# A hybrid trunk layer on one core: six small moves ahead of the MLP, a VectorE-only MLP passage, and another order of the second MLP product

## The chip, the cores and the metric

The kernel runs on one core of a Trainium2 chip. The metric is the device time of one execution in microseconds (us), the median of several runs. PE is TensorE's matmul side, PEld its weight loads, DVE is VectorE, ACT is ScalarE, POOL is GpSimd, SP issues nearly all the DMAs.

## The reference

One layer for 1024 prompt tokens and 8 x 16 sample tokens, 1152 in all, model width 1024, fp32:

```python
x = layer_norm(x, ln_in_g, ln_in_b)
proj = x @ w_in                      # 1024 -> 5920, split among four head groups
# A: Mamba-2 SSD with a causal conv of width 4     B: mLSTM, 4 heads
# C: RG-LRU, 512 channels, causal conv             D: gated linear attention (GLA), 4 heads
x = layer_norm(alpha * x + concat(A, B, C, D) @ w_out, ln1_g, ln1_b)
hid = square(relu(x @ w1 + b1))      # 1024 -> 4096
x = layer_norm(alpha * x + hid @ w2 + b2, ln2_g, ln2_b)
```

The outputs are x for prompt and sample tokens and eight recurrent states for each.

## The kernel before, in words

Every fp32 product is computed in three passes: an operand is split into a rounded part (`hi`, a copy on ACT) and the rest (`lo`, a subtraction on DVE), and `mm3` multiplies hi by hi, hi by lo and lo by hi into one PSUM bank. A split of a 128 x 1024 weight tile is thus one ACT copy and one DVE subtraction.

The stages follow each other: `dense_first` (input LayerNorm, transposes, the first three blocks of w_in, one of 384 token columns at a time), the rest of the input projection with the four mixers' steps woven in by `tick()` (every 12 matmuls a tick runs as many pending steps as the ticks left call for), the out-projection `dense_tm` in five groups of w_out rows, the first MLP product, and the second.

Both MLP products use a scheme of seven products of half-size blocks in place of eight, with sums and differences of blocks as operands. For the first, `x_first` and `x_rest` split the token side (tiles `xo`: A11, A12, then S1 to S4 and A22; the sums stand in `s` and in place in `x`) and `q_prep` the weights (tiles `wq`, split into `wo`: B11, B21, T1, T2, T3, T4, B22). `mlp_a(j)` runs the two products that need only A11 and A12, `mlp_b(j)` the other five. The stretch between the out-projection and the end of `x_rest(3)`, in which `mlp_a(0)` to `mlp_a(3)` run while the sums are made, is called the passage here. Its sums and splits are shared by DVE and POOL: the difference in place of `x`, the `lo` parts of S3 and A22 and all `wq` differences are POOL's.

The second product takes its operands from DRAM (`hid_d`, the sums `s_d`, the weight sums `t_d`) in units (p, u): product p, 256 rows u of the contraction. `load_to` and `prep_to` fetch four and split three units ahead. All eight product slots run over u = 0 to 5 first (`CHUNKS[0]`), then over u = 6, 7 as the tail; product slot 0 feeds the sample tokens only. The evacuated parts collect in `a1`, `a5`, `a6`, and in the rows `top`, `bot`, `smp`, which start as the residual (`res_make`, on POOL). The tail ends tile by tile with product 5, then 7, then 4, and the second LayerNorm (`ln_stats2`, `ln_a`, `ln_b`, `ln_g`, `ln_c`, `ln_stt`) is spread over DVE, ACT and POOL.

The order on each engine is made by a list scheduler from the program order and its priorities (`tc.high_priority()`); in the last stretch and in the first (`pinned`) program order is kept. Each engine then runs its list strictly in order. Large tiles come from one pool of 38 slots (`S`), the PSUM banks from a pool of 3 (`pd`) and one of 5 (`pm`).

All engine calls are made through one helper, so every row shows its line, L66 in the kernel before and L62 in the changed one.

Of the kernel before, what the change touches and what calls it, by code (L numbers as in the profile page):

```python
# [13 lines left out]
P = 128  # L14
NTOK = 1152
NT = 9
# [23 lines left out]
STT = (7, 6)  # L40
NG5 = 0
PIN = 'VATG'
LOG = ((4, 0), (4, 1))
CHUNKS = (tuple(range(6)), (6, 7))
# [6 lines left out]
def tile_trunk(ctx: ExitStack, tc: tile.TileContext, I, O, dbg=None):  # L51
# [665 lines left out]
    def conv_block(store, key, st_in, nrow, ch0, wcol, bcol, act, o_p, o_s, early=False):  # L717
# [11 lines left out]
        def evac(c, ps):  # L729
            if c == 0:  # L730
                raw = S("raw", (P, SW))
                d["raw"] = raw
                V.memset(raw[:, 0:3], 0.0)
                sv = raw[:, 1027:1179].rearrange("p (b s) -> p b s", s=19)
                d["sv"] = sv
                cs = d["cs"] if early else load()
                pt = pm("pcs")
                T.transpose(pt[:, 0:24], cs[0:24, :], ident[0:24, 0:24])
                A.activation(sv[:, :, 0:3], pt[:, 0:24].rearrange("p (b j) -> p b j", j=3), AF.Copy)
            raw = d["raw"]  # L740
# [36 lines left out]
        def state():  # L777
            raw, sv = d["raw"], d["sv"]
            cs = Dt("cso", 27)
            A.activation(cs[:, 0:3], raw[:, PT:PT + 3], AF.Copy)  # L780
            A.activation(cs[:, 3:27].rearrange("p (b j) -> p b j", j=3), sv[:, :, LS:LS + 3], AF.Copy)
            pt = pm("pco")
# [298 lines left out]
    def ml_steps(h):  # L1081
# [22 lines left out]
        def stB(i):  # L1104
# [41 lines left out]
            y = Dt("y", P)  # L1146
            A.activation(y, ti[:, 0:P], AF.Square, scale=r[:, 0:1], accum_out=r[:, 1:2])
# [3 lines left out]
            G.tensor_scalar(y, ti[:, 0:P], r[:, 3:4], None, op0=OP.mult)  # L1151
            d["y", i] = y
# [36 lines left out]
        for s in range(NT + 3):  # L1189
            def f(s=s):  # L1190
# [6 lines left out]
                if 3 <= s <= NT + 2:  # L1197
                    stC(s - 3)
# [97 lines left out]
    def gl_steps(p):  # L1296
# [21 lines left out]
        def stB(i):  # L1318
# [3 lines left out]
            if i < 8:  # L1322
# [11 lines left out]
                if i:  # L1334
                    G.tensor_scalar(St, St, sc[:, 1, i:i + 1], None, op0=OP.mult)
                    V.scalar_tensor_tensor(St, pS, sc[:, 2, i:i + 1], St, op0=OP.mult, op1=OP.add)
                else:
                    V.tensor_scalar(St, pS, sc[:, 2, 0:1], None, op0=OP.mult)
                if i < 7:
                    for h in range(2):  # L1340
                        hs = slice(64 * h, 64 * h + 64)
                        V.tensor_scalar(glB[hs, h, :], St[hs], sc[hs, 0, i + 1:i + 2], None, op0=OP.mult)
# [129 lines left out]
    def rg_steps(j):  # L1472
# [15 lines left out]
        def gates(c):  # L1488
            def f():
# [7 lines left out]
                if c < 2:  # L1497
                    split(c + 1)
# [45 lines left out]
        return [g0] + [w] * 5 + [gates(0)] + [w] * 0 + [gates(1)] + [w] * 0 + [gates(2), e1, e2, e3]  # L1544
# [86 lines left out]
    def w2_sums():  # L1631
# [3 lines left out]
        for k in range(KF // 2):  # L1635
            for c in (0, 256):
# [17 lines left out]
                def f3(sub=sub, store=store):  # L1654
# [3 lines left out]
                    sub("21", "22", "21")  # L1658
# [133 lines left out]
    def x_split(name, k, src, e=V):  # L1792
# [3 lines left out]
        e.tensor_tensor(t[:, 1, :], src, t[:, 0, :], op=OP.subtract)  # L1796
# [5 lines left out]
    def x_rest(k):  # L1802
# [31 lines left out]
    def q_prep(j):  # L1834
# [7 lines left out]
        def sub(dst, a, b):  # L1842
            G.tensor_tensor(wq[dst, j], wq[a, j], wq[b, j], op=OP.subtract)
# [126 lines left out]
    for g, n in enumerate(GR):  # L1970
# [4 lines left out]
        for i in range(NT):  # L1975
# [65 lines left out]
    mlp_a(0, firsts(1))  # L2041
    q_first(2)
    rest_cm(0, 1)
    x_rest(0)
    mlp_a(1, firsts(2))
    q_first(3)
    rest_cm(2)
    x_rest(1)
    q_load(0)
    mlp_a(2, firsts(3))  # L2050
    rest_cm(3)
    prep[0].pop(0)()
    x_rest(2)
    prep[0].pop(0)()
    q_load(1)
    mlp_a(3, lambda: None)
    prep[0].pop(0)()
# [37 lines left out]
    order, order_end = (1, 5, 6, 4, 0, 7, 2, 3), (2, 3, 0, 1, 6, 5, 7, 4)  # L2095
    tail = CHUNKS[-1]
    units = [(p, u) for us in CHUNKS for p in (order_end if us is tail else order) for u in us]
# [32 lines left out]
    def lo_engine(p, u):  # L2130
        return G if (p, u - tail[0]) in LOG else V

    def w_prep(i):
        if i < len(units):
            p, u = units[i]
            opw[p, u] = parts(wr.pop((p, u)), lo_engine(p, u))

    def a_prep(i):
        if i < len(units):
            p, u = units[i]  # L2140
            if prods[p][0]:
                opa[p, u] = parts(ar.pop((p, u)), lo_engine(p, u))
# [18 lines left out]
    def sample(p, u):  # L2161
        if p in samp:
            h, g = samp[p]
            (ah, al), (wh, wl) = hs[u // 2], opw[p, u]
            for k in range(2):
                n = (u % 2) * 2 + k
                mm3(sps[h], (ah[:, g, n], al[:, g, n]), (wh[:, k], wl[:, k]),
                    u == k == g == 0, u == NU - 1 and k == 1 and g == 0)

    acc = {}  # L2170

    def part_of(p, t):

        nm, ix = {1: ("a1", None), 5: ("a5", None), 6: ("a6", None), 2: ("top", 0), 3: ("top", 1), 4: ("bot", 0),
                  7: ("bot", 1)}[p]
        key = (nm, t // 2 if ix is None else t)
        if key not in acc:
            acc[key] = S3(nm)
        return acc[key][:, t % 2 if ix is None else ix, :]

    def evac(p, t, ps, first):
        a = part_of(p, t)
        if first and p in (1, 5, 6):
            if t % 2:
                V.tensor_copy(a, ps)
            else:
                A.activation(a, ps, AF.Copy)
        else:
            V.tensor_tensor(a, a, ps, op=OP.subtract if p == 4 else OP.add)
# [10 lines left out]
    def res_make(i):  # L2200
        r = row(i)
        G.tensor_tensor(r, r, ga, op=OP.mult)
        G.tensor_tensor(r, r, ba, op=OP.add)
        if 4 <= i < 8:
            G.tensor_tensor(r[:, left], r[:, left], r[:, right], op=OP.subtract)
# [20 lines left out]
    def ln_b(i):  # L2226
        rs = lnrs[i]
# [225 lines left out]
```

## Time and profile before

| | us |
|---|---|
| median of 3 runs | 1825.93 (1824.7 to 1827.39) |
| profiled execution | 1824.16 |
| its span, first to last instruction | 1822.4 |
| PE busy in the span | 1739.7 (95%) |
| DVE busy | 1220.2 (67%) |
| ACT busy | 748.3 (41%) |
| POOL busy | 598.9 (33%) |

Busy time is the sum of an engine's instructions in the span. Matmuls overlap in the pipeline and their ends are modelled, so idle time of PE, and what ended it, says more than its busy share: where PE is busy all the time a change on another engine can gain nothing, and where PE waits, the engine that ended the wait is the one to look at. The granted TensorE clock of the whole span is 0.986 of full speed.

### The profile page before, as it was taken

To read this page: it belongs to the slowest core of one execution; us is meant where nothing else is said; L and a number is where in the kernel's file an instruction comes from. 1 tells how busy PE (TensorE), PEld (TensorE's weight loads), DVE (VectorE), ACT (ScalarE), POOL (GpSimd) and SP (SyncE) were. 2 spreads that over 40 slices of the span, in tenths; PEclk is the share of its full clock that TensorE was granted. 3 is DMA by queue.
4 is the path that set the end of the run, shared out by engine and by line. 5 is a ranking of instruction groups with operands and counts; after the bars stand their busy time and mean duration, and the time that the engine had idled before them with its cause. 6 is when DMAs were issued, how large, how long until landed. Compare 5 with 4: busy or idle time off the path is not lost. (4 is left out here: it accounts for less than half of the span.)

```text
span 1822.4 us, 28131 instructions
## 1 busy us (share of the span) xinstructions
PE 1739.7 (95%) x10439; PEld 1580.7 (87%) x10439; DVE 1220.2 (67%) x2263; ACT 748.3 (41%) x1463; POOL 598.9 (33%) x558
## 2 busy tenths in 40 slices
PE   6999999999999999998999998999999999999995
PEld 5898989999989889897887888999999988888884
DVE  6867776644573654678777579666666678856569
ACT  4544433332341322365542275444444443433331
POOL 1123223522531313234255026433333135430047
PEclk8999999999999999999999999999999999999998
DMA  5132343546434350211445222554443696664542
GB/s 167 49 108 62 106 126 91 182 150 182 150 109 142 108 146 12 78 39 61 160 131 187 76 93 82 186 180 167 145 145 128 220 324 212 214 235 164 186 150 93
DMA packets 226961, 252.53 MB, mean 139 GB/s; under 512 B 27834, under 2 KB 171340, under 8 KB 226824
## 3 DMA queue, kind: packets, MB, share of 16 engines
q1 hardware_dynamic: 213000, 215.08, 37.4%
q10 hardware_dynamic: 13824, 35.66, 5.1%
q8 instruction: 82, 1.34, 0.3%
q14 instruction: 55, 0.45, 0.1%
HBM read 172.59 MB, written 76.33 MB: 137 GB/s over the span
## 5 line engine op out<-in xcount | busy, mean ns | idle before, releaser
L66 PE MATMUL pd<-xh,wh 128*128 128x384 f32 x936 | 330.1, 353 | 2.6 <-ACT xh L66 2.3
L66 PE MATMUL pd<-xh,wl 128*128 128x384 f32 x936 | 318.7, 340 | 0.0
L66 PE MATMUL pd<-xl,wh 128*128 128x384 f32 x936 | 311.0, 339 | 0.3 <-DVE xl L66 0.3
L66 PE MATMUL pm<-xo,wo 128*128 128x288 f32 x1680 | 232.2, 297 | 9.3 <-DVE wo L66 6.1
L66 PEld LDWEIGHTS pm<-xo,wo 128*128 128x128 f32 x1680 | 227.1, 190 | 10.7 <-DVE wo L66 7.3
L66 PEld LDWEIGHTS pd<-xh,wh 128*128 128x128 f32 x936 | 177.8, 190 | 8.4 <-ACT xh L66 3.3
L66 PEld LDWEIGHTS pd<-xl,wh 128*128 128x128 f32 x936 | 177.2, 190 | 1.9 <-issue 1.0
L66 PEld LDWEIGHTS pd<-xh,wl 128*128 128x128 f32 x936 | 177.2, 189 | 0.1
L66 POOL TENSOR_TENSOR wq<-wq 128x512 f32<-128x512 f32 x64 | 94.5, 1477 | 168.6 <-DVE wo L66 152.6
L66 PE MATMUL pd<-xo,wo 128*128 128x288 f32 x1008 | 140.3, 296 | 0.1
L66 PEld LDWEIGHTS pd<-xo,wo 128*128 128x128 f32 x1008 | 136.8, 189 | 0.3 <-ACT hid L66 0.3
L66 DVE TENSOR_TENSOR wo<-wq,wo 128x512 fp32r<-128x512 f32 x112 | 102.0, 930 | 31.3 <-ACT wo L66 30.6
L66 DVE TENSOR_TENSOR ol<-w2r,oh 128x1024 fp32r<-128x1024 f32 x62 | 97.9, 1586 | 26.5 <-ACT oh L66 10.0
L66 DVE TENSOR_TENSOR wl<-wr,wh 128x1024 fp32r<-128x1024 f32 x63 | 87.6, 1392 | 26.3 <-ACT wh L66 17.9
L66 ACT ACTIVATE oh<-ar 128x1024 fp32r<-128x1024 f32 x56 | 59.2, 1057 | 105.1 <-DVE ol L66 29.1
L66 DVE TENSOR_TENSOR ol<-ar,oh 128x1024 fp32r<-128x1024 f32 x54 | 78.1, 1446 | 33.1 <-ACT oh L66 28.8
L66 ACT ACTIVATE oh<-w2r 128x1024 fp32r<-128x1024 f32 x64 | 67.2, 1052 | 58.6 <-DVE ol L66 31.4
L66 PE MATMUL pd<-oh,ol 128*128 128x512 f32 (+1 forms) x228 | 89.5, 392 | 0.0
L66 PE MATMUL pd<-ol,oh 128*128 128x512 f32 (+1 forms) x228 | 89.3, 392 | 0.0
L66 PE MATMUL pd<-oh 128*128 128x512 f32 (+1 forms) x228 | 89.0, 391 | 0.0
L66 PE MATMUL pm<-oh,ol 128*128 128x512 f32 (+1 forms) x224 | 87.8, 392 | 0.0
L66 PE MATMUL pm<-ol,oh 128*128 128x512 f32 (+1 forms) x224 | 87.6, 391 | 0.0
(420 smaller groups left out, 4019.6 us busy)
## 6 DMA issues: line engine op xcount, KB each, us to landing
wr<-in_w_in_dram SPq DMA_DIRECT2D x46, 512.0 KB
wq<-in_mlp_w_dram SPq DMA_DIRECT2D x72, 256.0 KB
hid_d<-hid ACTq DMA_DIRECT2D x32, 576.0 KB
w2q<-in_mlp_w_dram SPq DMA_DIRECT2D x128, 128.0 KB
t_d<-w2q SPq DMA_DIRECT2D x128, 128.0 KB
s_d<-sq ACTq DMA_DIRECT2D x64, 256.0 KB
w2r<-in_mlp_w_dram SPq DMA_DIRECT2D x32, 512.0 KB
w2r<-t_d SPq DMA_DIRECT2D x32, 512.0 KB
```

The source lines that it names most:

```text
L66: r = f(*a, **k)
```

## The change

Ahead of the MLP: (1) in the conv blocks the transposition of the cached conv state (`pcs`, from the tile `cst`) runs with the third token block, not the first; (2) the conv's outgoing state is copied right after its last taps (`kept`), not in the step that transposes it; (3) in the mLSTM the transposition of a tile's output (`py`) comes four steps behind its first step, not three, the square goes into the PSUM bank `pb`, and the scaled output stays in `ti` where there was a tile `y`; (4) the GLA's state update gets high priority; (5) in the RG-LRU the second split of the gate input is issued a step earlier; (6) the weight sums' last difference has its sign turned, and the product that uses it is added, not subtracted.

The MLP passage: all sums and splits of the token side run on DVE, also the `wq` differences of the first two weight blocks; B11 and B21 of blocks 0 and 1 are split during the last group of the out-projection, and blocks 2 and 3 one product earlier than before. The ticks of the last group find their count used up, so the pending transpositions run in two batches.

The second product: products 1 and 2 over all eight u, then 6 and the sample-only 0 in turn, then 5 and 3, then 4 and 7 over u = 0 to 4, and as the tail 7 and 4 over u = 5 to 7, tile by tile, each row finished while the next tile is multiplied. Residual, sums and LayerNorm products run on DVE; POOL keeps the reciprocal root.

```diff
@@ conv_block
-                cs = d["cs"] if early else load()
-                pt = pm("pcs")
-                T.transpose(pt[:, 0:24], cs[0:24, :], ident[0:24, 0:24])
...
+            if c == 2:
                 pt = pm("pcs")
+                T.transpose(pt[:, 0:24], d["cs"][0:24, :], ident[0:24, 0:24])
...
-            st += [taps(c, 0, 2), taps(c, 2, 4)]
+            st += [taps(c, 0, 2), taps(c, 2, 4) if c < 2 else lambda c=c: (taps(c, 2, 4)(), kept())]
@@ mLSTM
-            y = Dt("y", P)
-            A.activation(y, ti[:, 0:P], AF.Square, scale=r[:, 0:1], accum_out=r[:, 1:2])
+            A.activation(pb[:, 0:P], ti[:, 0:P], AF.Square, scale=r[:, 0:1], accum_out=r[:, 1:2])
...
-        for s in range(NT + 3):
+        for s in range(NT + 4):
...
-                if 3 <= s <= NT + 2:
-                    stC(s - 3)
+                if 4 <= s <= NT + 3:
+                    stC(s - 4)
@@ RG-LRU
-        return [g0] + [w] * 5 + [gates(0)] + [w] * 0 + [gates(1)] + [w] * 0 + [gates(2), e1, e2, e3]
+        return [g0] + [w] * 4 + [lambda: split(1), gates(0)] + [w] * 0 + [gates(1)] + [w] * 0 + [gates(2), e1, e2, e3]
@@ x_rest
-        G.tensor_tensor(a21, a11, a21, op=OP.subtract)
+        V.tensor_tensor(a21, a11, a21, op=OP.subtract)
         x_split("S2", k, s12[:, 1])
-        x_split("S3", k, a21, G)
-        x_split("A22", k, a22, G)
+        x_split("S3", k, a21)
+        x_split("A22", k, a22)
@@ q_prep
-            G.tensor_tensor(wq[dst, j], wq[a, j], wq[b, j], op=OP.subtract)
+            (V if j < 2 else G).tensor_tensor(wq[dst, j], wq[a, j], wq[b, j], op=OP.subtract)
@@ last group of the out-projection
                 if i == 0:
                     q_first(0)
                     q_first(1)
+                    prep = {j: q_prep(j) for j in range(KF // 2)}
+                if i in (2, 3, 5, 6):
+                    prep[i // 4].pop(0)()
+                if i == 4:
+                    q_first(2)
+                if i == 7:
+                    q_load(0)
                     ticks_left[0] = 16
...
-                if i == 6:
-                    prep = {j: q_prep(j) for j in range(KF // 2)}
-                    prep[0].pop(0)()
-                    prep[0].pop(0)()
@@ second product
-units = [(p, u) for us in CHUNKS for p in (order_end if us is tail else order) for u in us]
+    tail = (5, 6, 7)
+    units = ([(p, u) for p in (1, 2) for u in range(NU)] + [(p, u) for u in range(NU) for p in (6, 0)]
+             + [(p, u) for p in (5, 3) for u in range(NU)] + [(p, u) for p in (4, 7) for u in range(tail[0])]
+             + [(p, u) for p in (7, 4) for u in tail])
...
         r = row(i)
-        G.tensor_tensor(r, r, ga, op=OP.mult)
-        G.tensor_tensor(r, r, ba, op=OP.add)
+        V.tensor_tensor(r, r, ga, op=OP.mult)
+        V.tensor_tensor(r, r, ba, op=OP.add)
...
+    def first(t):
+        ps = bank()
+        tile_prod(ps, 7, t)
+        add(acc["bot", t][:, 1], ps)
+        ln_stats2(4 + t, right)
+        add(acc["bot", t][:, 0], ps)
...
+    for t in range(4):
+        first(t)
+        if t:
+            ln_c(3 + t, left)
+            ln_c(3 + t, right)
+        second(t, lh if t == 3 else (left,))
+        if t < 3:
+            ln_b(4 + t)
+    ln_b(7, left)
+    ln_stt(7, right, 0)
+    ln_stt(7, right, 1)
+    ln_c(7, left)
```

The order on PE in `dense_first`, at the end of the first token block. `pd` is a projection's bank, `pcs` the bank for the transposed conv state, `cst` its source. Before:

```order
L66 MATMUL pd<-xh_103,wl 128x384
L66 MATMUL pd<-xl_111,wh 128x384
L66 MATMUL pcs<-ident,cst 128x24
L66 MATMUL pd<-xl_111,wh 128x384
L66 MATMUL pcs<-ident,cst 128x24
L66 MATMUL pd<-xh_96,wh 128x384
```

The same place on PE in the changed kernel:

```order
L62 MATMUL pd<-xh_103,wl 128x384
L62 MATMUL pd<-xl_111,wh 128x384 x2
L62 MATMUL pd<-xh_96,wh 128x384
L62 MATMUL pd<-xh_96,wl 128x384
L62 MATMUL pd<-xl_104,wh 128x384
```

The two transpositions are gone from between the projections; they now stand after the third token block.

The order on DVE in the passage, the first `x_rest` (k = 0), before:

```order
L66 TENSOR_TENSOR s_11213<-x_0_10823,x_4_10836 128x576
L66 TENSOR_TENSOR s_11213<-s_11213,x_0_10823 128x576
L66 TENSOR_TENSOR x_4_10836<-x_4_10836,s_11213 128x576
L66 TENSOR_TENSOR xo<-s_11213,xo 128x576 x2
L66 TENSOR_TENSOR xo<-x_4_10836,xo 128x576
L66 TENSOR_TENSOR hid<-pd,hid 128x288 x2
L66 TENSOR_TENSOR wo<-wq,wo 128x512 x2
```

And in the changed kernel:

```order
L62 TENSOR_TENSOR s_11199<-x_0_10793,x_4_10800 128x576
L62 TENSOR_TENSOR s_11199<-s_11199,x_0_10793 128x576
L62 TENSOR_TENSOR x_0_10793<-x_0_10793 128x576
L62 TENSOR_TENSOR x_4_10800<-x_4_10800,s_11199 128x576
L62 TENSOR_TENSOR xo<-s_11199,xo 128x576 x2
L62 TENSOR_TENSOR xo<-x_0_10793,xo 128x576
L62 TENSOR_TENSOR xo<-x_4_10800,xo 128x576 x2
L62 TENSOR_TENSOR wo<-wq,wo 128x512
```

DVE has nine operations of 576 columns for each k where it had six; POOL has none.

The order on DVE at the very end, before (`g`, `bb` are the second LayerNorm's vectors):

```order
L66 TENSOR_TENSOR res<-res,pm 128x256
L66 BN_STATS st<-res 128x6
L66 BN_AGGR st<-st 128x2
L66 TENSOR_SCALAR rs<-st 128x1
L66 SCALAR_TENSOR_TENSOR res<-res,st,g_17257 128x512 x2
L66 TENSOR_TENSOR res<-res,bb_17259 128x1024 x2
L66 SCALAR_TENSOR_TENSOR res<-res,rs,bb_17259 128x512 x2
L66 SCALAR_TENSOR_TENSOR res<-res,st,g_17257 128x512 x2
L66 SCALAR_TENSOR_TENSOR res<-res,rs,bb_17259 128x512 x2
```

And in the changed kernel:

```order
L62 TENSOR_TENSOR res<-res,pd 128x256
L62 BN_STATS st<-res 128x6
L62 BN_AGGR st<-st 128x2
L62 TENSOR_SCALAR rs<-st 128x1
L62 SCALAR_TENSOR_TENSOR res<-res,st,g_16539 128x512
L62 SCALAR_TENSOR_TENSOR res<-res,rs,bb_16541 128x512
L62 TENSOR_TENSOR res<-res,g_16539 128x512
L62 TENSOR_TENSOR res<-res,bb_16541 128x512
```

Behind the last statistics stand four operations of 512 columns, all of the last row, where there were eight of 512 and two of 1024 for four rows.

## Rows read from the trace of the kernel before

**Rows 1.** Waits of PE, longest first: total us, times, longest.

```profile
PE py L66 <- POOL y L66: 7.3, 9, 2.4
...
PE pm L66 <- DVE wo L66: 6.1, 3, 2.4
PE pcs L66 <- DMA cst<-in_state_ssd_conv_dram: 5.8, 1, 5.8
...
PE pb L66 <- DVE E L66: 3.6, 6, 1.3
...
PE pgt L66 <- DVE gxl L66: 2.6, 3, 1.2
...
PE pb L66 <- DVE glB L66: 2.0, 3, 1.4
...
PE pco L66 <- ACT cso L66: 1.5, 1, 1.5
```

**Rows 2.** Busy us of PE, PEld, DVE, ACT, POOL in one window; clock.

```profile
1500.00:1550.00 50.00, 50.00 (x219) 40.70 (x217) 41.58 (x24) 18.11 (x19) 26.70 (x10) 1.00 0.60 211
```

**Rows 3.** Timeline of PE at the start: start, length, operation, [idle before].

```profile
25.72 0.34 PE L66 MATMUL pd<-xh,wl 128*128 128x384 f32 x1
25.90 0.33 PE L66 MATMUL pd<-xl,wh 128*128 128x384 f32 x1
32.03 0.27 PE L66 MATMUL pcs<-ident,cst 24*128 24x24 f32 x1 [5.80 <-DMA cst<-in_state_ssd_conv_dram]
...
38.75 0.82 PE L66 MATMUL pt<-ident,x 128*128 128x128 f32 x6
```

**Rows 4.** Timeline of DVE in the same stretch: the last token tile's normalisation.

```profile
29.83 0.81 DVE L66 TENSOR_SCALAR x<-x,rs 128x1024 f32<-128x1024 f32 x1
```

**Rows 5.** Timeline of PE at the start of the passage.

```profile
1071.18 6.53 PE L66 MATMUL pm<-xo,wo 128*128 128x288 f32 x48
1077.54 1.91 PE L66 MATMUL pt<-ident,acc 128*128 128x128 f32 x16
```

**Rows 6.** Timeline of DVE in the passage.

```profile
1058.34 1.43 DVE L66 TENSOR_TENSOR xo<-x,xo 128x576 fp32r<-128x576 f32 x2
...
1080.32 0.76 DVE L66 TENSOR_TENSOR s<-x,x 128x576 f32<-128x576 f32 x1 [2.12 <-ACT x L66]
...
1081.90 1.87 DVE L66 TENSOR_TENSOR x<-x,s 128x576 f32<-128x576 f32 x1
...
1123.37 0.45 DVE L66 TENSOR_TENSOR hid<-pd,hid 128x288 f32<-128x288 f32 x1
1123.74 0.68 DVE L66 TENSOR_TENSOR wo<-wq,wo 128x512 fp32r<-128x512 f32 x1
```

**Rows 7.** Timeline of POOL in the passage.

```profile
1081.16 2.00 POOL L66 TENSOR_TENSOR x<-x 128x576 f32<-128x576 f32 x1 [1.91 <-DVE s L66]
```

**Rows 8.** The second product's lo parts on DVE: min/median/max ns, first and last start.

```profile
L66 DVE TENSOR_TENSOR ol<-w2r,oh x61: 1207/1219/3451, 1453.6 to 1760.6; 128x1024 fp32r<-128x1024 f32 x61
```

**Rows 9.** Groups of POOL in the second product: count, busy us, mean ns.

```profile
L66 POOL TENSOR_TENSOR res<-res,ba 128x1024 f32<-128x1024 f32 x9 | 28.6, 3175 | 9.0 <-DVE ba L66 8.3
```

**Rows 10.** Timeline of ACT as the second product's first unit is split.

```profile
1434.19 1.06 ACT L66 ACTIVATE oh<-ar 128x1024 fp32r<-128x1024 f32 x1 [0.33 <-DMA ar<-hid_d]
```

**Rows 11.** Timeline of PE: its last matmul.

```profile
1802.39 0.28 PE L66 MATMUL pm<-oh,ol 128*128 128x256 f32 x1
```

**Rows 12.** Timeline of DVE after it.

```profile
1807.35 0.41 DVE L66 TENSOR_TENSOR res<-res,pd 128x256 f32<-128x256 f32 x1
...
1809.46 3.56 DVE L66 SCALAR_TENSOR_TENSOR res<-res,st,g 128x512 f32<-128x512 f32 x2
...
1817.86 1.40 DVE L66 SCALAR_TENSOR_TENSOR res<-res,rs,bb 128x512 f32<-128x512 f32 x2
```

**Rows 13.** Timeline of POOL in the tail: the reciprocal root.

```profile
1805.76 0.55 POOL L66 TENSOR_TENSOR rs<-rs,nhalf 128x1 f32<-128x1 f32 x1 [1.07 <-DVE rs L66]
```

**Rows 14.** Timeline of ACT in the tail: one row normalised.

```profile
1806.71 1.24 ACT L66 ACTIVATE res<-res,rs 128x1024 f32<-128x1024 f32 x1 [0.74 <-POOL rs L66]
```

More of the change, by code (lines that the diff above doesn't have):

```diff
@@ L1335, in stB @@
                     G.tensor_scalar(St, St, sc[:, 1, i:i + 1], None, op0=OP.mult)
[L1336 to L1342, printed above, removed]
+                with tc.high_priority():
+                    if i:
+                        V.scalar_tensor_tensor(St, pS, sc[:, 2, i:i + 1], St, op0=OP.mult, op1=OP.add)
+                    else:
+                        V.tensor_scalar(St, pS, sc[:, 2, 0:1], None, op0=OP.mult)
+                    if i < 7:
+                        for h in range(2):
+                            hs = slice(64 * h, 64 * h + 64)
+                            V.tensor_scalar(glB[hs, h, :], St[hs], sc[hs, 0, i + 1:i + 2], None, op0=OP.mult)
             else:
@@ L2167, in sample @@
                 mm3(sps[h], (ah[:, g, n], al[:, g, n]), (wh[:, k], wl[:, k]),
-                    u == k == g == 0, u == NU - 1 and k == 1 and g == 0)
+                    u == k == g == 0, u == NU - 1 and k == g == 1)
     acc = {}
[L2172 to L2189, printed above, removed]
     def row(i):
@@ new lines, in add, with part, evac @@
+    def add(dst, a):
+        V.tensor_tensor(dst, dst, a, op=OP.add)
+    def part(nm, t):
+        key = (nm, t // 2)
+        if key not in acc:
+            acc[key] = S3(nm)
+        return acc[key][:, t % 2, :]
+    def evac(p, t, ps):
+        if p in (1, 6, 5):
+            x = part(f"a{p}", t)
+            if p == 1:
+                A.activation(x, ps, AF.Copy)
+            else:
+                V.tensor_tensor(x, part("a1" if p == 6 else "a6", t), ps, op=OP.add)
+        top, bot = acc.get(("top", t)), acc.get(("bot", t))
+        if p == 2:
+            add(top[:, 0], ps)
+            later.append(lambda: (add(top[:, 0], part("a1", t)), ln_stats2(t, left)))
+        elif p == 6:
+            later.append(lambda: add(bot[:, 0], x))
+        elif p == 5:
+            later.append(lambda: add(top[:, 1], x))
+            later.append(lambda: add(bot[:, 1], x))
+        elif p == 3:
+            add(top[:, 1], ps)
+            later.append(lambda: (ln_stats2(t, right), ln_a(t)))
+            later.append(lambda: ln_b(t))
+            later.append(lambda: ln_c(t, left))
+            later.append(lambda: ln_c(t, right))
+        elif p == 4:
+            add(bot[:, 0], ps)
+        elif p == 7:
+            add(bot[:, 0], ps)
+            add(bot[:, 1], ps)
@@ L2315, in tile_trunk @@
             V.tensor_tensor(ba, ba, b2, op=OP.add)
[L2316 to L2320 removed]
+        if i % 3 == 1:
+            if i > 1 and made:
+                res_make(made.pop(0))
+            if todo:
+                res_load(todo.pop(0))
+        if p == 5 and u == 0:
             g2 = vec_bc("g2", I["ln2_g"][0])
@@ L2323, in tile_trunk @@
         sample(p, u)
-        if end and p == 5:
-            break
+        for _ in range(2):
+            if later:
+                later.pop(0)()
         if not p:
             continue
-        if cu == 0:
+        if u == 0:
             banks = [bank() for _ in range(4)]
         (ah, al), (wh, wl) = opa[p, u], opw[p, u]
+        n = NU if p in (1, 2, 6, 5, 3) else NU - len(tail)
         for k in range(2):
```

218 lines of the change are left out of this document (69 added, 149 removed).

## The prediction

> **What bounds the kernel now.** I read the page's busy line first: PE is busy 1739.7 of a span of 1822.4 us, the next engine 1220.2. So 82.7 us are all that PE doesn't work in, and a change on another engine counts only where PE waits. The waits of PE, grouped by who ended them, came next [rows 1]: the ones this change touches are small and many, py after POOL 7.3 us in nine, pm after the weight splits wo 6.1, one wait of 5.8 for the conv state's DMA, pb after E 3.6, pgt 2.6, pb after glB 2.0, pco 1.5. Then a table of windows over the MLP: from 1500 to 1550 PE is busy 50.00 of 50 at clock 1.00, beside DVE 41.58, ACT 18.11, POOL 26.70 [rows 2]. The second product is PE's alone, and another order in it gains nothing; it can only lose. At the end PE stops at 1802.67 [rows 11], 19.7 before the span's end: nothing but the last rows' LayerNorm and their DMAs stands there. Three places are thus left: the waits in front, the MLP passage, the tail.
>
> **Start.** PE multiplies until 26.2, then stands 5.80 for the cached conv state, until 32.03 [rows 3]. Behind the first pcs stand 18 matmuls of the first block (counted in the order), then the transposes of the next token tiles, which in before begin at 38.75. Two losses lie in that: the wait, and the pace after it. The 18 take the 6.7 us from 32.03 to 38.75, 0.37 each, where two in a row started 0.18 apart before the wait (25.72, 25.90): twice as long, the lower of the clock's two levels after an idle stretch. With pcs gone from here, 18 x 0.18 from 26.2 ends at 29.4. The transposes need the last token tile of the next block, which DVE finishes at 30.64 [rows 4]. So they begin near 30.7 in place of 38.75: 8.0 gained. This is not the 5.8 of the wait list. Bounds: 9.3 if that tile is not needed yet (29.4), 4 if something else of the third tile is late or the clock falls in the new 1.3 us gap. The state is needed with the third token block, long after its DMA.
>
> **mLSTM.** py goes four steps behind its first step in place of three. A tick is 12 matmuls of 384 columns, 2.1 us at 0.18; the longest of the nine py waits is 2.4 [rows 1], so one step more covers nearly all. I take 5.0 of 7.3. I don't take all because a head now has 14 steps and the same ticks: two ticks hold two steps, and there pb waits for E, at most 1.3 each time; and the square into pb holds that bank longer. Ends: 2 and 7.3.
>
> **Other waits in front.** The outgoing conv state is copied a step before its transposition: 1.5 of 1.5. High priority for the GLA state: 1.5 of glB's 2.0. pgt waits for the split that now comes a step earlier: 1.3 of 2.6, since DVE itself may be behind. The sign in the weight sums moves nothing. Bounds of the three together: 1 and 6.1.
>
> **The passage.** Here DVE decides: PE's waits for wo are its last [rows 1]. The row to see is one difference of 576 columns: two of them take 1.43, so 0.72 each, and 0.76 for a first one, while the one that runs beside POOL takes 1.87 [rows 6]; POOL's own takes 2.00 [rows 7]. And DVE waits for POOL's results in turn. In the changed kernel POOL does nothing here before the second pair of weight blocks. From the first sum at 1080.3, DVE then has, up to the split of T4 of the first block: 36 operations of 576 columns (nine for each of four k) x 0.72 = 25.9; six wo and two wq of 512 columns x 0.68 = 5.4; eight hid x 0.45 = 3.6 [rows 6]. That is 34.9, to 1115.2. In before this split ends at 1123.74 + 0.68 = 1124.4. Gain 9.2; I take 9.0. PE bounds it from above: 48 matmuls of 288 columns in 6.4 us are 0.1325 each, and the 11 runs of 24 such matmuls in this stretch, counted in the order, x 24 x 0.1325 = 35.0 and 32 transposes at some 0.1 = 3.3 [rows 5] from 1071.2 end at 1109.5, so no more than 14.4. Below, the moved work adds fully: 12 differences x 0.72 + 5 wq x 0.68 = 12 lost. I take the first since the two rows of one form, 0.72 and 1.87, are from the same passage and differ by POOL alone. The early splits of blocks 0 and 1 go into the out-projection's last group, where they pass no queue that PE waits for; what they cost is under the costs below.
>
> The Trainium skill's "Perfetto Trace Analysis", section "Optimizing Scalar/DVE Operations", says that work of a saturated DVE may be offloaded, even to GpSimd, and adds that the two share a read port, so that it might not help. Its first half speaks against this change and would give the 12 lost; its second half for it, and the 1.87 against 0.72 agrees with that half. By the first half the sum below would be 14 in place of 35.
>
> **Second product.** Nothing, 0: PE is full, DVE has 8.4 of 50 free [rows 2]. POOL's residual operations go to DVE: nine with ba at 3.2 on POOL [rows 9] and nine with ga, 18 x 1.22 (the time of an undisturbed 128 x 1024 DVE operation, [rows 8]) = 22 us, spread over 350. Against it, the lo parts that now reach 3.45 beside POOL fall to 1.22. Three units are prepared ahead. If that cover is gone, it costs as in rival C.
>
> **Tail.** Let E be the end of the last matmul. Before: 19.7. After: the last tile ends with product 7, then 4. Product 4's 36 half matmuls of 256 columns at 0.12 (0.1325 x 256/288) take 4.3, so product 7's bank is free at E - 4.3. DVE then does an add of 512, the statistics of the right half and another add, together 2.1, and four operations of 512 columns for the row before, 2.5 at some 0.65: until E + 0.3. Two adds of 256, statistics, aggregation and the small step take 2.1, as from 1807.35 to 1809.46 [rows 12]: E + 2.4. POOL's root, two steps, 0.55 + 0.3 [rows 13]: E + 3.3. One row on ACT is 1.24 [rows 14], its half at most 0.7: E + 4.0. The two left operations of 512 on DVE, 0.70 each (1.40 for two in [rows 12]), E + 5.4. From the last DVE operation to the span's end are 3.1 (1819.26 to 1822.4): E + 8.6. The two STT of the right half run beside ACT. Gain 19.7 - 8.6 = 11.1. In before the same chain carried four rows, and two STT took 3.56 beside POOL against 1.40 [rows 12]. Ends: 8 (the 3.56 pace once more, one more row behind) and 12.2.
>
> **Costs with no row.** Two double steps in the mLSTM, a bank held longer, transposes in two batches at the end of the out-projection (a batch waits for its copies), product switches in the second product. Nearest: PE waits of 1 to 2.4 [rows 1]. I take 2.4, one of the longest; ends 0 and 8.
>
> **Sum.** 8.0 + 5.0 + 1.5 + 1.5 + 1.3 + 9.0 + 11.1 - 2.4 = 35.0. The profiled execution took 1824.16, so 1789.2; the median of the runs lies 1.8 above it, and stays so: 1791.
>
> **Rivals.**
> A: in the passage the moved operations add fully, since DVE was the bound there and still is. For it: PE waits for DVE, not POOL [rows 1]. Against: 1.87 against 0.72 [rows 6]. 1791 + 9 + 12 = 1812.
> B: the waits in front are replaced, not removed: start 4, py 2, the other three 2. For it: E and gxl sit on the same DVE right beside them [rows 1]. Then 9.3 of the front's 17.3 go: 1800.
> C, slower: the second product loses its lookahead. The 38 slots now hold 24 for the tail's operands, whose units are three, not two, rows of the contraction, and the sample operands stay until product 3. A unit whose tiles come late is prepared in series, two hi on ACT at 1.06 [rows 10] and two lo on DVE at 1.22 [rows 8]: 4.6 of PE. It turns at 35 / 4.6, about 8 of the 58 units ahead of the tail; 12 to 20 of them, from the first of products 5 and 3 on, give 1846 to 1883. Against: three units in hand, and before fed PE without a gap from the same pool.
> D: about seven late units, 32 us: no change, 1823.
>
> **Chances.** Forecast 0.73, with its own range 1783 to 1798 (start 4 to 9.3, py 2 to 7.3, tail 8 to 12.2 and the costs 0 to 8 do not all fall one way). B 0.12, A 0.06, C 0.06, D 0.03. 0.2% is 3.7 us, about what a measurement of this kernel can tell. Faster are the forecast, B and A, 0.91, of which I give 0.01 to a C that comes on top of either: 0.90; same is D, 0.03; slower is C, 0.07. The range for 8 in 10 takes in the forecast, B, and A nearly, and below the gain's upper ends (the passage 14.4, start 9.3, py 7.3): 1779 to 1811.
>
> **What would show it.** At 26 us PE goes on, no wait for cst, and matmuls keep 0.18 until the transposes near 31. py is gone from the waits or below 2.5. In the passage every 576-column operation on DVE takes 0.72 to 0.76, POOL stands, and T4's split ends some 44 us after the passage's first product starts, in place of 53. In the second product windows PE stays at 50 of 50, and no lo part passes 1.3. The span ends 8 to 9 after the last matmul. It is wrong if PE shows idle stretches of several us between 1420 and 1760, if new waits with E, pb or transposed tiles fill what py left, or if wo waits stay at 6.

## The result, and the profile after

The changed kernel takes 1800.11 us (median of 4, 1799.21 to 1801.39), the kernel before 1825.88 beside it: a ratio of 0.9861, 95% interval 0.9846 to 0.9876, 25.8 us. Forecast were 1791, 35 less, and a range of 1779 to 1811. The direction and the range hold; the gain is 9 us short. But the median lies outside the forecast's own narrower range, 1783 to 1798, and is the time of rival B, 1800.

The page's first part of the changed kernel, with its span of 1799.2 (23.2 shorter in the profiled executions):

```profile
PE 1733.6 (96%) x10445; PEld 1576.5 (88%) x10445; DVE 1180.1 (66%) x2307; ACT 749.2 (42%) x1459; POOL 439.9 (24%) x490
```

POOL lost a quarter of its work. PE is busy 6.1 us less, beside a granted clock that rose from 0.986 to 0.993 over the span; the other 17.1 of the 23.2 are idle time of PE. Matmuls of one form can be counted in both traces, and the starts of the same one compared. That gives a ledger by stage (us; "this stage" is the change in "ahead" from the row above):

| the same point | before | after | ahead | this stage | forecast |
|---|---|---|---|---|---|
| 120th matmul of the input projection | 51.1 | 43.0 | 8.1 | +8.1 | +8.0 |
| its 930th, ahead of the mLSTM | 310.2 | 300.9 | 9.4 | +1.3 | +1.5 |
| its 1449th, in the mLSTM's third head | 456.8 | 450.6 | 6.2 | -3.2 | |
| its 1580th, the same head | 494.8 | 494.4 | 0.4 | -5.8 | |
| its 1800th, end of the mLSTM | 554.3 | 549.1 | 5.2 | +4.7 | +5.0 for all three |
| its last, end of the GLA | 851.3 | 845.9 | 5.4 | +0.2 | +1.5 and 1.3 |
| 1st matmul of the MLP, start of the passage | 1071.2 | 1068.5 | 2.7 | -2.8 | -2.4 |
| its 400th | 1142.2 | 1129.3 | 12.9 | +10.2 | +9.0 |
| end of the last matmul | 1802.7 | 1789.4 | 13.3 | +0.4 | 0 |
| end of the span | 1822.4 | 1799.2 | 23.2 | +9.9 | +11.1 |

Start, passage and tail are as forecast within 1.2 us each. The mLSTM lost 4.2 where it was to gain 5.0: that is 9.2 of the 11.8 by which the ledger (23.2) is short of the forecast (35). Some expectations below were written from points that lie a few matmuls apart: their 3.1, 9.5, 10.0 and 10.6 are 2.8, 7.8, 10.2 and 10.3 where the same matmuls are compared. The waits of PE show where the time went (total, times, longest):

```profile
PE pb L62 <- DVE E L62: 9.5, 5, 6.0
...
PE pgt L62 <- DVE gxl L62: 2.5, 3, 1.1
PE pb L62 <- DVE glB L62: 2.5, 2, 1.5
...
PE pm L62 <- ACT wo L62: 2.2, 2, 2.1
PE py L62 <- POOL ti L62: 1.6, 2, 0.9
PE pS L62 <- POOL wv L62: 1.5, 1, 1.5
PE pd L62 <- DVE ol L62: 1.3, 1, 1.3
PE py L62 <- DVE c L62: 1.3, 2, 0.6
...
PE pm L62 <- DVE wo L62: 1.0, 1, 1.0
```

Against [rows 1]: pcs and pco are gone, wo fell from 6.1 to 1.0, and py from 7.3 to 2.9, since to the 1.6 after POOL come two new waits of the same transposition, 1.3 together, that the view puts down to DVE's c. pgt and glB stand where they were. But E rose from 3.6 to 9.5, with one wait of 6.0, where the longest for E in before is 1.3. The timelines of PE, DVE and SP around it:

```profile
452.35 0.34 PE L62 MATMUL pd<-xh,wl 128*128 128x384 f32 x1
458.68 0.80 PE L62 MATMUL pb<-va,E 128*128 128x129 f32 x2 [5.99 <-DVE E L62]
...
460.35 0.52 PE L62 MATMUL pd<-xh,wl 128*128 128x384 f32 x1
460.67 0.52 PE L62 MATMUL pd<-xh,wh 128*128 128x384 f32 x1
```

```profile
457.41 0.42 DVE L62 TENSOR_TENSOR w2q<-w2q 128x256 f32<-128x256 f32 x1 [4.92 <-DMA w2q<-in_mlp_w_dram]
457.75 0.41 DVE L62 TENSOR_SCALAR mlo<-mlo,pscl 128x384 f32<-128x384 f32 x1
458.08 0.34 DVE L62 SCALAR_TENSOR_TENSOR E<-Mb,TM,posm 128x128 f32<-128x128 f32 x1
```

```profile
446.79 0.46 SPq L1074 DMA_DIRECT2D Mb<-mrow_d  x1
447.35 0.38 SPq L1077 DMA_DIRECT2D c<-in_state_mlstm_C_dram  x1
447.82 1.07 SPq L169 DMA_DIRECT2D wr<-in_w_in_dram  x1
448.95 4.51 SPq L1644 DMA_DIRECT2D w2q<-in_mlp_w_dram  x1
453.55 4.63 SPq L1650 DMA_DIRECT2D t_d<-w2q  x4
```

Read from the bottom: SP issues the cached state c and a weight block, and then stands 4.51 in the issue of one small load for the weight sums. DVE reaches that sum in its list and stands 4.92 for it; E is two places behind; PE waits 5.99 for E. In before SP has a standstill of the same size in the same place, but there it falls on a store:

```profile
451.56 0.42 SPq L1076 DMA_DIRECT2D c<-in_state_mlstm_C_dram  x1
452.09 0.61 SPq L173 DMA_DIRECT2D wr<-in_w_in_dram  x1
452.79 4.18 SPq L1648 DMA_DIRECT2D t_d<-w2q  x1
```

PE has no wait there in before. In the changed kernel the wait costs more than itself: the matmuls behind it start 0.32 apart (460.35, 460.67), where 0.17 to 0.18 is the pace elsewhere, and the window shows it in the clock (us, busy PE, PEld, DVE, ACT, POOL, clock):

```profile
450.00:500.00 50.00, 43.32 (x274) 41.59 (x273) 24.87 (x96) 16.27 (x54) 23.90 (x42) 0.93 0.46 139
```

In before this window has 47.89 of PE at clock 1.00. From the 1453rd matmul of the input projection to its 1464th the changed kernel loses 7.8: 6.0 of waiting and 1.8 at the lower pace.

The passage, in before and then in the changed kernel (the same columns):

```profile
1071.18:1142.21 71.03, 61.64 (x432) 60.12 (x431) 61.34 (x72) 42.50 (x73) 43.80 (x27) 0.93 0.31 99
```

```profile
1068.52:1129.31 60.79, 57.54 (x432) 56.58 (x431) 52.34 (x86) 40.14 (x71) 7.19 (x6) 1.00 0.33 107
```

DVE is busy 9.0 less with more operations. PE's idle time in it falls from 9.4 to 3.2, and the other 4.1 of the 10.2 are pace: the granted clock is 0.93 over the passage in before and 1.00 in the changed kernel.

### The profile page after: what moved, and what is told of

Read it like the earlier page. It is cut to its first block, busy times and chain, and to the rows that moved or that the text cites. A ratio compares the mean times of both kernels' runs of the same rounds, so it can differ in the third digit from the quotient of the medians.

```text
span 1799.2 us, 28086 instructions
## 1 busy us (share of the span) xinstructions
PE 1733.6 (96%) x10445; PEld 1576.5 (88%) x10445; DVE 1180.1 (66%) x2307; ACT 749.2 (42%) x1459; POOL 439.9 (24%) x490
## 5 line engine op out<-in xcount | busy, mean ns | idle before, releaser
L62 POOL TENSOR_TENSOR rs<-rs,nhalf 128x1 f32<-128x1 f32 x27 | 17.3, 642 | 423.8 <-DVE rs L62 420.3
L62 DVE TENSOR_TENSOR wo<-wq,wo 128x512 fp32r<-128x512 f32 x112 | 98.2, 894 | 34.4 <-ACT wo L62 33.7
L62 POOL TENSOR_TENSOR wq<-wq 128x512 f32<-128x512 f32 x56 | 81.1, 1449 | 156.8 <-DVE wo L62 127.6
L62 DVE TENSOR_TENSOR ol<-w2r,oh 128x1024 fp32r<-128x1024 f32 x64 | 77.9, 1219 | 34.6 <-ACT oh L62 21.1
L62 DVE TENSOR_TENSOR ol<-ar,oh 128x1024 fp32r<-128x1024 f32 x56 | 68.4, 1222 | 41.0 <-ACT oh L62 32.7
L62 DVE TENSOR_TENSOR w2q<-w2q 128x256 f32<-128x256 f32 x128 | 55.3, 435 | 51.8 <-DMA w2q<-in_mlp_w_dram 45.4
```

Of the source, the lines that this page charges most:

```text
L62: r = f(*a, **k)
```

## The experiments

Medians are given with the kernel before timed beside each group of four (1825.53, 1826.54, 1825.58).

**The mLSTM undone.** The changed kernel with three steps and the tile y again.

```diff
-            A.activation(pb[:, 0:P], ti[:, 0:P], AF.Square, scale=r[:, 0:1], accum_out=r[:, 1:2])
+            y = Dt("y", P)
+            A.activation(y, ti[:, 0:P], AF.Square, scale=r[:, 0:1], accum_out=r[:, 1:2])
...
-        for s in range(NT + 4):
+        for s in range(NT + 3):
```

> The changed kernel with its mLSTM part as before (py three steps behind, square into a tile y). In the changed kernel one wait of PE for E takes 6.0 us (458.7), because DVE stands 4.9 us before it in a weight sum whose load SP issued 4.5 us long, right behind the cached state c and a weight block. Theory 1: the 14th step shifted SP's order so that this load came behind c; with the step gone SP's order is that of before and the 6.0 wait and the half pace after it (9.5 in all) go, while py's waits (7.3) come back: the mLSTM is as long as before, 4.4 us shorter than in the changed kernel, 1795.7. Theory 2 (rival): the wait comes from the sign change in the weight sums or from the high priority in the GLA; then E keeps 6 us, py comes back, and the time is 1806 to 1808.

1798.54 (1794.9 to 1801.39), ratio 0.9854 (0.9839 to 0.9869); the profiled run is the fastest of them, 1794.9. Its waits:

```profile
PE py L62 <- POOL y L62: 7.4, 10, 2.4
...
PE pb L62 <- DVE E L62: 2.8, 5, 1.3
```

The long wait for E is gone and SP's list is in before's order again (c, wr, then a store); py's waits are back, at 7.4. From the 930th matmul to the 1800th it loses 0.2 on before, where the changed kernel loses 4.2. That the edit of py brought the wait for E is shown; the rival falls. All six traces here with this edit and c issued by SP ahead of its head have the wait, 5.5 to 6.2; the five with the mLSTM of before have none for E above 1.8. Which part of the edit does it, the step more or the square in pb, is not told apart. The median moved 1.6 only, less than its own spread, and the stage itself scatters with the clock: with the mLSTM of before it takes from 0.7 less to 3.3 more than in before's trace. So the edit is not shown to gain anything as it stands: it takes 4.4 out of py and puts 5.9 into E.

**c two steps later.** The same edit kept, the load of c moved.

```diff
-        D.dma_start(c0[:, :, 0:P], I["state_mlstm_C"][0][:, h].rearrange("b d v -> d b v"))
...
+                if s == 2:
+                    D.dma_start(ml["c0", h][:, :, 0:P], I["state_mlstm_C"][0][:, h].rearrange("b d v -> d b v"))
```

> The changed kernel with the load of the cached mLSTM state c issued in the third step of a head, not ahead of the head. Theory 1 (the long wait for E is SP's order at this place): no wait for E above 1.5 us, py stays near 1.6, the 9.5 us go: 1790 to 1792. Rival: the load finds another weight sum or weight block behind it, and DVE stands as long elsewhere: 1798 to 1802.

1794.91 (1793.94 to 1795.64), ratio 0.9835 (0.9822 to 0.9847): 5.2 below the changed kernel, the best median of all versions here. py stays at 1.7, but E keeps a wait of 3.2, and another of 2.13 appears at 374:

```profile
PE pb L62 <- DVE E L62: 7.4, 5, 3.2
```

The theory is right on the place and too large on the size. PE's waits in the whole mLSTM fall from 14.2 to 10.6, but its granted clock is 0.98 in place of 0.99, and in the trace that stage is only 1.0 shorter than in the changed kernel. Of the 5.3 between the two spans, 1.7 lie ahead of the mLSTM and 2.5 between its end and the passage, where the source is the same. That the median's 5.2 is this wait's is not shown.

**c issued by ACT.** To see whether c or the weight blocks hold SP's queue.

```diff
-        D.dma_start(c0[:, :, 0:P], I["state_mlstm_C"][0][:, h].rearrange("b d v -> d b v"))
+        A.dma_start(c0[:, :, 0:P], I["state_mlstm_C"][0][:, h].rearrange("b d v -> d b v"))
```

> The changed kernel with the load of the cached mLSTM state c issued by ACT, not by SP; in SP's list only that row is gone. With c moved two steps later the longest wait for E fell from 6.0 to 3.2 and the time to 1794.9; the weight-sum loads then stood behind weight blocks alone. Theory 1 (the rows of SP's queue right behind c are held until c has left): the longest wait for E is 3.3 or less, the time 1792 to 1796. Rival (the weight blocks wr alone hold the queue, c's place doesn't matter, and c_later gained by its shifted steps): E keeps 5 to 6 us and the time 1799 to 1801.

1798.79 (1796.24 to 1799.2), ratio 0.9845 (0.9831 to 0.9859). The place again, on SP and DVE:

```profile
445.90 0.38 SPq L169 DMA_DIRECT2D wr<-in_w_in_dram  x1
446.37 0.56 SPq L1644 DMA_DIRECT2D w2q<-in_mlp_w_dram  x1
447.02 7.16 SPq L1650 DMA_DIRECT2D t_d<-w2q  x4
```

```profile
453.42 0.42 DVE L62 TENSOR_TENSOR w2q<-w2q 128x256 f32<-128x256 f32 x1 [3.11 <-DMA w2q<-in_mlp_w_dram]
```

The load is now issued in 0.56, the standstill falls on the stores behind it, and PE waits 3.3 for E as expected. But DVE still waits until 453.4 for the load. So c ahead of it costs 2.7 of the 6.0; 3.3 remain with no c on SP's queue, behind the weight block. The time is 2.8 above the expectation's upper end, and only 1.3 below the changed kernel: that shows 2.7 of a wait less, and not where the rest of c_later's gain came from.

**E first.** E's operations at high priority.

```diff
+            with tc.high_priority():
                 V.scalar_tensor_tensor(E, ml["Mb", h][:, ts], TM[:, i, 24 + h:25 + h], posm[mi],
...
+            with tc.high_priority():
                 V.tensor_tensor(E, E, pa[:, 0:P], op=OP.mult)
```

> The changed kernel with E's operations at high priority and nothing else. In DVE's list at the start of the third head E still stands behind the weight sums, since its source comes last, but ahead of a split. Theory 1 (DVE is held in a weight sum by the DMA, and the order among DVE's ready operations doesn't help): the longest wait for E stays 5 to 6, the time 1798 to 1801. Rival (E waited for DVE's own work, the splits beside it): the wait falls below 3, 1794 to 1797.

1799.69 (1795.39 to 1801.74), ratio 0.9860 (0.9843 to 0.9878); the longest wait for E is 6.2. DVE stands 4.71 in the sum ahead of it, and between the sum and E lies one operation of 0.41, so E does not wait for DVE's own work: the rival falls. But at this place DVE's order is still sum, `mlo`, E, as in the changed kernel. The priority did not move E there, and what E ahead of the sum would be worth is not shown.

**POOL back in the passage.** The early splits kept.

```diff
-        V.tensor_tensor(a21, a11, a21, op=OP.subtract)
+        G.tensor_tensor(a21, a11, a21, op=OP.subtract)
...
-        x_split("S3", k, a21)
-        x_split("A22", k, a22)
+        x_split("S3", k, a21, G)
+        x_split("A22", k, a22, G)
...
-            (V if j < 2 else G).tensor_tensor(wq[dst, j], wq[a, j], wq[b, j], op=OP.subtract)
+            G.tensor_tensor(wq[dst, j], wq[a, j], wq[b, j], op=OP.subtract)
```

> The changed kernel with the passage's differences back on POOL as before (difference in place of x, lo parts of S3 and A22, all wq differences), the early splits kept. Theory 1 (the 10.0 us that the passage gained are DVE's slowdown beside POOL, 1.87 for 0.72): loses 8 to 12, 1808 to 1812, with DVE's 576-column operations at 1.5 to 1.9 beside POOL. Rival (the gain is the early splits of B11 and B21, which took 4 us of DVE's work out of the passage and let PE start on ready weights): loses under 4, 1800 to 1804.

1806.87 (1805.36 to 1807.47), ratio 0.9899 (0.9887 to 0.9912), 6.8 above the changed kernel; its passage gains 3.4 on before in place of 10.2. DVE in the first `x_rest`, here and then in the changed kernel:

```profile
1076.59 1.88 DVE L62 TENSOR_TENSOR x<-x,s 128x576 f32<-128x576 f32 x1
1078.39 2.66 DVE L62 TENSOR_TENSOR xo<-s,xo 128x576 fp32r<-128x576 f32 x2
1080.97 1.99 DVE L62 TENSOR_TENSOR xo<-x,xo 128x576 fp32r<-128x576 f32 x1
```

```profile
1079.99 0.75 DVE L62 TENSOR_TENSOR x<-x,s 128x576 f32<-128x576 f32 x1
1080.66 1.42 DVE L62 TENSOR_TENSOR xo<-s,xo 128x576 fp32r<-128x576 f32 x2
1082.00 2.09 DVE L62 TENSOR_TENSOR xo<-x,xo 128x576 fp32r<-128x576 f32 x3
```

With POOL, the four operations shown take 6.5 on DVE and leave POOL three; without it, six take 4.3. The passage of the changed kernel itself differs between traces: it gains 10.2 or 10.3 in four, and 8.8 or 8.9 in five in which the granted clock over it is 0.97 in place of 1.00. So 5.4 to 6.9 come from taking POOL out, beside which DVE is slower, and 3.4 stay with the earlier splits: under the expected 8 to 12, over the rival's 4.

**Only the passage, without early splits.** The same four lines changed in the kernel before.

```diff
-        G.tensor_tensor(a21, a11, a21, op=OP.subtract)
+        V.tensor_tensor(a21, a11, a21, op=OP.subtract)
...
-        x_split("S3", k, a21, G)
-        x_split("A22", k, a22, G)
+        x_split("S3", k, a21)
+        x_split("A22", k, a22)
```

> The kernel before with the passage's differences on DVE alone (those of x and the first two wq blocks) and nothing else; no early splits. With POOL put back in the changed kernel its passage gained 3.1 in place of 10.0, so POOL's share was 6.9. Theory 1 (the two parts add): the passage 6 to 8 shorter, 1818 to 1820. Rival A (without the early splits DVE is the bound, and its added work eats the gain): 0 to 3 shorter, 1823 to 1826.

1814.60 (1811.57 to 1818.58), ratio 0.9936 (0.9921 to 0.9951). In the trace the passage is 6.4 shorter, so the two parts add (6.4 and 3.4 against 8.8 to 10.3). The median is 3 to 5 lower than expected; the profiled run was already 3.5 ahead at the passage's start, in code that is the same, and the executions spread over 7 us. The term is shown by the trace, the size of the median isn't explained.

**Only pcs.** The start alone, in the kernel before.

```diff
-                cs = d["cs"] if early else load()
-                pt = pm("pcs")
-                T.transpose(pt[:, 0:24], cs[0:24, :], ident[0:24, 0:24])
...
+            if c == 2:
+                pt = pm("pcs")
+                T.transpose(pt[:, 0:24], d["cs"][0:24, :], ident[0:24, 0:24])
```

> The kernel before with one edit: pcs is transposed with the third token block. Theory 1 (the wait of 5.8 also cost the clock, 18 matmuls at 0.37 for 0.18): 8.0 to 8.7 faster, 1817.3. Rival (only the wait goes, or the later blocks give it back): 5.8 or less, 1820 and above.

1818.19 (1815.81 to 1820.56), ratio 0.9961 (0.9948 to 0.9974): 7.3 faster, between the two ranges. At the 120th matmul it is 8.6 ahead, more than the 5.8 of the wait, so the pace is part of it; by the end of the span 4.6 of the 8.6 are left in the profiled run. One new wait gives part of it back:

```profile
PE pco L66 <- ACT cso L66: 3.2, 1, 3.2
```

It was 1.5 [rows 1]; the outgoing state's copy is late for a PE that comes earlier. In the changed kernel the second edit takes that wait away. Another 2.5 go in the mLSTM, which is before's: its waits are no longer, but the granted clock there is 0.99 in place of 1.00.

**Ticks from the first tile.** For the 2.8 lost ahead of the passage.

```diff
                     q_first(1)
+                    ticks_left[0] = 16
                     prep = {j: q_prep(j) for j in range(KF // 2)}
...
                     q_load(0)
-                    ticks_left[0] = 16
```

> The changed kernel with the last group's count of ticks set to 16 at its first tile, as before, not at its eighth, so that the pending transpositions are spread again. Between the end of the mixers and the passage the change lost 3.1 us (5.8 ahead of before, then 2.7). Theory 1 (two batches of transpositions wait for their copies): 1.5 to 3 faster, 1797 to 1799, the passage starting that much earlier. Rival (the loss is in the waits prho and wl and the early splits on DVE, not in the batches): within 0.7 of the changed kernel, 1800.

1801.19 (1799.16 to 1801.68), ratio 0.9860 (0.9847 to 0.9874): nothing gained. In its trace 1.9 are lost in that stretch, but kernels whose source there is the changed kernel's lose from 0.8 to 2.8, so the two batches cost nothing that can be seen. What the 2.8 are stays open; in the changed kernel part of it is the clock behind a wait of 4.5 for wl that both kernels have, 0.93 from 850 to 900, where before has 0.97.

**The residual on POOL.**

```diff
-        V.tensor_tensor(r, r, ga, op=OP.mult)
-        V.tensor_tensor(r, r, ba, op=OP.add)
+        G.tensor_tensor(r, r, ga, op=OP.mult)
+        G.tensor_tensor(r, r, ba, op=OP.add)
```

> The changed kernel with the 18 operations that make the residual rows on POOL, as before. Theory 1 (the second product is PE's, and where POOL or DVE takes them is hidden): 0, within 1 us of 1800, although lo parts on DVE beside POOL reach 2 to 3.4 us. Rival (the move to DVE is worth something): 1802 to 1806, with PE waits for ol or res.

1811.39 (1808.69 to 1814.84), ratio 0.9920 (0.9906 to 0.9934): 11 lost where I had put 0. From the passage's end to the last matmul it loses 10.3 on before, in one place. POOL, DVE and PE there:

```profile
1454.45 8.50 POOL L62 TENSOR_TENSOR res<-res,ga 128x1024 f32<-128x1024 f32 x3 [29.42 <-DMA b<-in_mlp_b_dram]
1462.90 9.96 POOL L62 TENSOR_TENSOR res<-res,ba 128x1024 f32<-128x1024 f32 x3
```

```profile
1453.53 0.69 DVE L62 TENSOR_SCALAR ga<-ga 128x1024 f32<-128x1024 f32 x1 [8.05 <-DMA ga<-in_ln_g_dram]
...
1457.44 3.30 DVE L62 TENSOR_TENSOR ba<-ba,b 128x1024 f32<-128x1024 f32 x1
1460.66 3.36 DVE L62 TENSOR_TENSOR ol<-ar,oh 128x1024 fp32r<-128x1024 f32 x1
1463.95 3.36 DVE L62 TENSOR_TENSOR ol<-w2r,oh 128x1024 fp32r<-128x1024 f32 x1
```

```profile
1467.37 0.79 PE L62 MATMUL pd<-ol,oh 128*128 128x512 f32 x1 [8.00 <-DVE ol L62]
```

DVE stands 8.05 for the vector ga, with the lo parts of the next unit behind it in its list; then it takes 3.3 for each of three operations beside POOL, the last of which is the split that PE waits for. With the residual on DVE it stands 8.08 for ga too, but its operations then take 1.22 each, and the same place costs a wait of 1.3.

**Three rows on DVE, six on POOL.** Is it that place, or every POOL operation?

```diff
-        V.tensor_tensor(r, r, ga, op=OP.mult)
-        V.tensor_tensor(r, r, ba, op=OP.add)
+        e = V if i < 3 else G
+        e.tensor_tensor(r, r, ga, op=OP.mult)
+        e.tensor_tensor(r, r, ba, op=OP.add)
```

> The changed kernel with the residual operations of the first three rows on DVE as in it, and of the other six rows on POOL. With all nine on POOL the second product lost 10.6 us, in one wait for ol of 8.0 at 1467, where six POOL operations in a row lay beside the lo parts of the unit that PE needed next. Theory 1 (only that place is bare, the later units are three ahead): within 2 us of the changed kernel, 1799 to 1802. Rival (each POOL operation beside DVE costs PE something in the whole second product): 6 to 8 lost, 1806 to 1808.

1801.22 (1798.4 to 1801.59), ratio 0.9866 (0.9848 to 0.9883): the changed kernel's time within its spread, and one wait for ol of 1.39, at the same place. The other twelve operations on POOL cost nothing. Theory 1 holds: the product is covered by its units in hand, except at its start.

**Only the second product.** The changed product and tail in the kernel before.

```diff
-                    sub("21", "22", "21")
+                    sub("21", "21", "22")
...
+    tail = (5, 6, 7)
+    units = ([(p, u) for p in (1, 2) for u in range(NU)] + [(p, u) for u in range(NU) for p in (6, 0)]
```

> The kernel before with the changed second product, its tail and the sign of the weight sum, and nothing else. Theory 1 (what the trace shows of the two, 0.6 in the product and 9.9 in the tail, stands by itself): 10 to 11 faster, 1815.5. Rival (part of the tail's gain came from what the passage left on POOL and in the pool of tiles): 6 to 8, 1818 to 1820.

1817.00 (1811.5 to 1817.98), ratio 0.9952 (0.9935 to 0.9969): 8.6 faster. In its trace the product gains nothing and the tail 9.9, as in the changed kernel; the profiled run lost 2.9 ahead of it. The tail stands by itself; the rival's range isn't reached by the trace, the median lies between the two.

**Combined.** c later, E first, and the residual's vectors from the third unit on.

```diff
-        if i == 0:
+        if i == 2:
             ga = vec_bc("ga", I["ln1_g"][0], ALPHA)
```

> The changed kernel with the load of c two steps later (1794.9 alone), E's operations at high priority, and the vectors of the residual (ga, ba, b2) loaded from the third unit of the second product on, not from its first. Theory 1 (DVE's list is what holds E, and at 1461 us what holds the lo parts of the unit that PE waits for): no wait for E above 1.5, no wait for ol, 1790 to 1793. Rival (DVE meets the late weight-sum loads anyway, whatever E's rank; the 1.3 us at 1461 come from the unit's own DMA): 1794 to 1797.

1796.34 (1789.9 to 1798.59), ratio 0.9837 (0.9815 to 0.9859). The wait for ol is gone, and from the 400th matmul of the MLP to the last this kernel gains 2.0 on before in place of 0.4: there the theory holds. PE still waits 4.6 for E at its longest, so on E it falls, and the time lies in the rival's range. Better than the changed kernel, not told apart from c_later, whose runs lie closer together.

## Why the prediction was right or wrong

**Right in mechanism and size.** The start: 8.1 against 8.0. Both losses that the prediction named are gone, and the transposes now follow the projections with no gap.

```profile
27.28 0.44 PE L62 MATMUL pd<-xh,wl 128*128 128x384 f32 x1 [0.56 <-DVE wl L62]
...
30.19 0.34 PE L62 MATMUL pd<-xl,wh 128*128 128x384 f32 x1
30.37 1.12 PE L62 MATMUL pt<-ident,x 128*128 128x128 f32 x6
```

That the number fits so closely is in part luck: the prediction had PE done at 29.4 and idle until the last token tile at 30.64; in fact PE waited 0.56 for wl first and came to the transposes at 30.37. A forecast of 5.8 from the wait list alone would have missed more than a quarter; only_pcs bears that out. The passage: 10.2 against 9.0, with 0.75 for a DVE operation of 576 columns where 0.72 was taken. The sum counted DVE's time alone; the trace splits the gain into 6.1 of waits of PE and 4.1 of clock, for which the prediction had no term here. Its upper bound is a slip: 1124.4 less 1109.5 is 14.9, not 14.4. From the passage on to the last matmul: 0.4 against 0. Rival A fell by pool_in_passage. Rival C, the lost lookahead, shows in no wait but the 1.3 at 1461.

The outgoing conv state: its wait of 1.5 is gone, as forecast. The costs: -2.4 against the -2.8 ahead of the passage, but by luck, since ticks_first shows nothing of the transposes in two batches that the term named. The 1.8 that was added for the median did not stay: the changed kernel's profiled execution, 1800.95, lies 0.8 above its median.

**Right with a wrong size.** The tail, 9.9 against 11.1. Its chain, the last matmul ending at 1789.37:

```profile
1789.81 0.41 DVE L62 TENSOR_TENSOR res<-res,pd 128x256 f32<-128x256 f32 x1
...
1791.85 0.15 DVE L62 TENSOR_SCALAR rs<-st 128x1 f32<-128x1 f32 x1
1791.92 0.74 DVE L62 SCALAR_TENSOR_TENSOR res<-res,st,g 128x512 f32<-128x512 f32 x1
1792.09 0.98 POOL L62 TENSOR_TENSOR rs<-rs,nhalf 128x1 f32<-128x1 f32 x1 [7.84 <-DVE rs L62]
...
1793.17 0.82 POOL L62 TENSOR_SCALAR rs<-st,rs 128x1 f32<-128x1 f32 x1
1794.02 0.81 ACT L62 ACTIVATE res<-res,rs 128x512 f32<-128x512 f32 x1 [8.49 <-POOL rs L62]
...
1795.59 0.69 DVE L62 TENSOR_TENSOR res<-res,bb 128x512 f32<-128x512 f32 x1
```

DVE's part is 0.2 late. POOL's two steps take 0.98 and 0.82 in place of the 0.55 and 0.3 that I took: they lie beside the two operations on the row's other half that I had called covered. Those two operations cost no time themselves, but POOL's steps grew by 1.0 beside them.

**Wrong.** The step "I take 5.0 of 7.3" in the mLSTM. py's own waits did go, from 7.3 to 2.9, 4.4 of the 5.0. What failed is the price beside it, "there pb waits for E, at most 1.3 each time": one wait for E took 6.0, and 7.8 with the clock. With the 14th step 71 loads of the weight sums stand ahead of this c on SP's queue where before and py_undone have 72, and the 72nd is the one that stands behind it; DVE, which runs its list in order, stands in that sum with E behind it. The prediction had named these loads in no term, and its bounds of 2 to 7.3 held only the waits of the edit itself. py_undone shows that the edit brings this wait; c_on_act that c's place is 2.7 of its 6.0; the rest of the chain is read from the orders of SP and DVE. Whether the wait of 1.54 for wv is the double step that the prediction named stays open: it is in all six traces with the edit and c issued by SP ahead of its head, and in none of the three in which c is issued elsewhere.

So the prediction's own sign of being wrong, new waits for E that fill what py left, is what happened, and the measured 1800 is rival B's time: waits in front replaced, not removed. B's mechanism holds for the mLSTM, pgt and glB. Its 1800 is met by luck all the same, since the start gained 8.1, not B's 4, the mLSTM lost 4.2 where B still gained 2, and the ledger's 23.2, short of the 25.7 that B leaves of the 35, is made up for by where the median lies.

The steps "1.3 of 2.6" for pgt and "1.5 of glB's 2.0" failed: pgt keeps 2.5, glB rose to 2.5, and the stage gained 0.2 of 2.8. An earlier split and a higher priority didn't reach the operation that ends these waits; no run here looks further.

The step "18 x 1.22, spread over 350" for the residual came out at 0, but for a reason that I had not seen: residual_on_pool shows that in the new order these operations on POOL cost 10.3. The windows of before [rows 2] were read from the middle of the product, where three units are in hand, and not from its first 30 us, where a wait for a vector and the next unit's split stand in one list.

## What to carry to other kernels

When an edit adds or removes a step in a loop that also paces loads, follow each load's neighbours on the issuing queue and the operation that stands behind its consumer in the in-order list; the cost of the edit can lie there, outside the waits it removes. Price a wait of PE with the pace of the matmuls behind it, and a DVE operation by whether POOL runs beside it; and read the cover of a long product at its start, not in its middle.

## What the runs showed of the hardware

A DVE operation on two tiles of 576 columns takes 0.75 alone and 1.88 to 1.99 beside POOL; one of 1024 columns 1.22 and 3.36. POOL's operation on a single column took 0.98 beside a DVE operation on SBUF tiles, and, in the one place read for it, 0.55 beside a DVE addition from a PSUM bank (1805.76 in before, [rows 13], with DVE's `res<-res,pd` at 1805.60). On SP's queue the issue of a 128 KB load took 4.51 right behind two of 512 KB, where 120 of the 128 such issues take 0.3 to 0.6, and the store in its place in before 4.18. Behind the same wait of 2.1 in the passage the granted clock falls in five traces and stays in four, which is worth 1.4. Executions of one program spread by 1.7 us (c later) to 8.7 us (combined) in groups of four to six. The ledger of one execution shows the place of a loss where medians do not, but the same code of one stage still takes up to 1.5 (the passage) or 4.0 (the mLSTM) longer in one trace than in another.
